# Differential attention in an encoder layer: the second softmax's factor computed on GpSimd instead of VectorE, and other planned waits around it

## The chip, the cores and the metric

The kernel runs on one core of a Trainium2 chip. The metric is the device time of one execution in microseconds (us); lower is better. The engines of the core are named as in the profile: PE is TensorE's matmul pipe, PEld its weight loads, DVE is VectorE, ACT is ScalarE, POOL is GpSimd and SP is SyncE, which here only issues transfers.

## The reference

One layer of an encoder trunk with 512 tokens and 1024 channels: a norm, one wide input projection, three branches (pooling, differential attention, a bidirectional recurrence) with gates, an output projection, then a SwiGLU feed-forward network and a final norm. The change lies in the attention branch alone:

```python
def diff_attention(q, k, v, lam, gain, lambda_init):
    # 4 heads, each with 2 softmaxes over 512 keys; query blocks of 128
    ...
        s = jnp.einsum('bqhcd,bkhcd->bhcqk', qblk, k) * scale
        s = s - slopes[:, None, None, None] * dist
        p = jax.nn.softmax(s, axis=-1)
        a = (p[:, :, 0] - lam * p[:, :, 1]).astype(v.dtype)
        return jnp.einsum('bhqk,bkhe->bqhe', a, v)
    ...
    o = rms_norm(o, gain) * (1.0 - lambda_init)
```

For each query row there are two sums of exponentials, z0 and z1. The kernel does not divide by z0 at this point: it forms e0 - lam * (z0 / z1) * e1 from the unnormalised exponentials e0 and e1, and lets 1/z0 enter later, inside the head's norm. The number -lam * z0 / z1, one for each row, is "the second softmax's factor"; in the code it is `co`.

## The kernel before, in words

Every matmul is done as three fp32r products of a high and a low part, so each weight block that arrives by DMA is split first: ACT writes the high part (`whi`, line 183) and DVE the low part (`wlo`, line 184). Both must be there before PE can use the block.

The attention stage works on four heads, and in each on four blocks of 128 queries. `scores(i)` (line 1046) issues, for each of the two softmaxes, two matmuls into a PSUM bank; one DVE operation adds the distances and takes the minimum (line 1056); one ACT operation takes the exponential and its row sum, which lands in `zz` (line 1058). Then DVE takes the reciprocals of the two sums (line 1062, `rr`), forms the factor (line 1064, `co`) and combines the two exponentials (line 1066). `turn(i)` (line 1069) transposes the result on PE in four pieces, and ACT and DVE copy it out of PSUM as high and low part (`aT`, lines 1075 and 1076). After four blocks, 12 matmuls multiply with the values (line 1097), and `head_norm` (line 647) squares the result, sums it with four small matmuls by `onesD` (line 657), passes through three small DVE operations, one power on POOL (line 140, called from line 666) and one more DVE operation, and ends with four transposes of `rso` (line 671).

The order of the matmuls is made when the program is built. Several generators run side by side under a planner (`Pipe`, line 39): the four heads, the pooling windows, and the stream of other jobs (`jobs.stream`: the projections of later heads, of the pooling branch `u`, and the `ups` of the recurrence), which fills the time between. A planned clock advances by a fixed price at each matmul (line 95) and transpose (line 100); a generator that yields `("w", t)` is taken up again t planned us later, and one that yields `("e", name, t)` waits until an event is marked. Waiting heads come before the job stream in the list, so a head goes on as soon as its wait is over, and the job stream takes what lies between. The job stream gives up control after every second matmul. PE keeps the order that the planner makes. The order on ACT, DVE and POOL is fixed at build time too, by a scheduler that models when each instruction becomes ready; on the chip each of these queues runs strictly in that order.

The waits of a head stand in lines 1080 and 1085: from one `turn` to the next `scores` 1.8, from `scores(i + 1)` to `turn(i)` 1.6. When the attention stage's job stream is used up, the next stage (line 1735: the pooling branch's mix, the gates' sums and differences `gsum`, and gate jobs) follows on PE.

Of the kernel before, what the change touches and what calls it, by code (L numbers as in the profile page):

```python
# [11 lines left out]
F32 = mybir.dt.float32  # L12
# [3 lines left out]
ALU = mybir.AluOpType  # L16
PSUM = bass.MemoryType.PSUM

P = 128
S = 512  # L20
D = 1024
NB = S // P
# [16 lines left out]
class Pipe:  # L39
# [8 lines left out]
    def mark(self, name):  # L48
        self.events[name] = self.t
# [27 lines left out]
def encoder_kernel(ctx: ExitStack, tc: tile.TileContext, x, norm1_g, w_in, pool_w, pool_scale,  # L77
# [3 lines left out]
    nc = tc.nc  # L81
# [3 lines left out]
    def pool(name, bufs=1, **kw):  # L85
        return tc.tile_pool(name=name, bufs=bufs, **kw)


    def mm(out_, lhsT, rhs, start, stop, chain=False):
        i = nc.tensor.matmul(out_, lhsT=lhsT, rhs=rhs, start=start, stop=stop, skip_group_check=chain)  # L90
        tc.keep_in_program_order(i)
        n = 1
        for d in rhs.shape[1:]:
            n *= d
        pipe.t += max(0.107, n * 0.0004167 + 0.002) if rhs.dtype == F32R else max(0.216, n * 0.001667 + 0.004)

    def transpose(out_, in_, idn):
        tc.keep_in_program_order(nc.tensor.transpose(out_, in_, idn))  # L98
        pipe.t += 0.108
# [8 lines left out]
    const = ctx.enter_context(pool("const"))  # L108
    wraw = ctx.enter_context(pool("wraw", 2))
    wsp = ctx.enter_context(pool("wsp", 3))  # L110
    small = ctx.enter_context(pool("small", 5))
    psum = ctx.enter_context(pool("psum", 3, space=PSUM))

    def bank(name, shape=(P, 512)):
        return psum.tile(list(shape), F32, name=name, bufs=2 if name == "tp" else 3)
# [7 lines left out]
    warmed = nc.scalar.activation(out=warm, in_=warm, func=AF.Exp).ins  # L123
    ident = const.tile([P, P], F32, name="ident")
    make_identity(nc, ident)
    onesD = const.tile([P, 1], F32, name="onesD")
    nc.vector.memset(onesD, 1.0 / P)
    mhalf = const.tile([P, 8], F32, name="mhalf")
    nc.vector.memset(mhalf, -0.5)
    masks = const.tile([P, len(LEVELS), P], U8, name="masks")  # L130
    vcol = const.tile([P, 14], F32, name="vcol")
    gain_a = const.tile([P, 1], F32, name="gain_a")
    lb = const.tile([P, 8], F32, name="lb")
    om = const.tile([P, 8], F32, name="om")
    nlam = const.tile([P, 1], F32, name="nlam")
# [3 lines left out]
    def pow_mhalf(dst, src):  # L139
        return nc.gpsimd.tensor_tensor(out=dst, in0=src, in1=mhalf[:, :src.shape[1]], op=ALU.pow).ins  # L140

    def rsqrt_eps(dst, mean):

        ms = small.tile([P, 8], F32, name="ms")[:, :mean.shape[1]]
        eng = nc.vector if mean.space == PSUM else nc.gpsimd
        eng.tensor_scalar(out=ms, in0=mean, scalar1=1.0, scalar2=EPS, op0=ALU.mult, op1=ALU.add)
        return pow_mhalf(dst, ms)
# [431 lines left out]
    ps = bank("mm")  # L579
# [67 lines left out]
    def head_norm(o_ps, tmp, gain, r0=None, bufs=2):  # L647


        og = tmp.tile([P, S], F32, name="og", bufs=bufs)  # L650
        sq = tmp.tile([P, S], F32, name="sqo", bufs=bufs)
        nc.scalar.activation(out=sq, in_=o_ps, func=AF.Square)
        nc.scalar.activation(out=og, in_=o_ps, func=AF.Copy, scale=gain)
        yield ("w", 1.3)
        sp = bank("tp")
        for b in range(NB):
            mm(sp[:, b:b + 1], sq[:, b * P:(b + 1) * P], onesD, True, True)
        r = small.tile([P, NB], F32, name="rso")
        if r0 is None:
            rsqrt_eps(r, sp[:, 0:NB])  # L660
        else:
            m = small.tile([P, NB], F32, name="mo")
            nc.vector.tensor_tensor(out=m, in0=sp[:, 0:NB], in1=r0, op=ALU.mult)
            nc.vector.tensor_tensor(out=m, in0=m, in1=r0, op=ALU.mult)
            nc.vector.tensor_scalar(out=m, in0=m, scalar1=EPS, scalar2=None, op0=ALU.add)
            pow_mhalf(r, m)
            nc.vector.tensor_tensor(out=r, in0=r, in1=r0, op=ALU.mult)
        yield ("w", 3.55)
        rb = bank("tp")
        for b in range(NB):  # L670
            transpose(rb[:, b * P:(b + 1) * P], r[:, b:b + 1].to_broadcast([P, P]), ident)
        return og, rb
# [359 lines left out]
    def att_head(h):  # L1032
        if h:
            yield ("e", f"QK{h - 1}", 0.0)
        if h > 1:
            yield ("e", f"AN{h - 2}", 0.0)
        yield ("e", f"AF{h}", 6.0)
        t = att.pop(h)
        at, (vh, vl), aT, y_attn = ATT["at"], ATT["v"], ATT["aT"], ATT["y"]
        strip = ATT["strip"].tile([P, 896], F32, name="strip")  # L1040
        nc.sync.dma_start(out=strip, in_=c_dist[h])
        zz = at.tile([P, NB, 2], F32, name="zz")
        rr = at.tile([P, NB, 2], F32, name="rr")
        probs = {}

        def scores(i):
            bs = slice(i * P, (i + 1) * P)
            mx = small.tile([P, 2], F32, name="mx")
            ex = []
            for c in range(2):  # L1050
                ps = bank("rc")
                mm(ps, t[f"q{c}"][:, bs], t[f"k{c}"], True, False)
                mm(ps, t[f"q{c}"][:, bs], t[f"l{c}"], False, True)
                s = at.tile([P, S], F32, name=f"s{c}")

                nc.vector.tensor_tensor_reduce(out=s, in0=strip[:, 384 - P * i:896 - P * i], in1=ps, scale=1.0,  # L1056
                                               scalar=3.0e38, op0=ALU.add, op1=ALU.min, accum_out=mx[:, c:c + 1])
                nc.scalar.activation(out=s, in_=s, func=AF.Exp, scale=-1.0, bias=mx[:, c:c + 1],  # L1058
                                     accum_out=zz[:, i, c:c + 1])
                ex.append(s)  # L1060

            nc.vector.reciprocal(out=rr[:, i, :], in_=zz[:, i, :])
            co = small.tile([P, 1], F32, name="co")
            nc.vector.scalar_tensor_tensor(out=co, in0=zz[:, i, 0:1], scalar=nlam, in1=rr[:, i, 1:2],
                                           op0=ALU.mult, op1=ALU.mult)
            nc.vector.scalar_tensor_tensor(out=ex[0], in0=ex[1], scalar=co, in1=ex[0], op0=ALU.mult, op1=ALU.add)  # L1066
            probs[i] = ex[0]

        def turn(i):
            bs = slice(i * P, (i + 1) * P)  # L1070
            p = probs.pop(i)
            pt = bank("tp", (P, NB, P))
            for k in range(NB):
                transpose(pt[:, k, :], p[:, k * P:(k + 1) * P], ident)
            nc.scalar.copy(out=aT[0][:, :, bs], in_=pt)
            nc.vector.tensor_tensor(out=aT[1][:, :, bs], in0=pt, in1=aT[0][:, :, bs].bitcast(F32), op=ALU.subtract)

        scores(0)
        for i in range(NB):
            yield ("w", 1.8 + (0.7 if i == 0 else 0.0))  # L1080
            if i + 1 < NB:
                scores(i + 1)
            else:
                mark(f"QK{h}")
            yield ("w", 1.6 + (1.0 if i + h == 0 else 0.0))
            if h and i == 0:
                yield ("e", f"PV{h - 1}", 0.0)
            turn(i)
        mark(f"T{h}")
        yield ("e", "VA", 1.5)  # L1090
        yield ("w", 1.5)
        ps = bank("rc")
        es = slice(h * P, (h + 1) * P)
        terms = [(vh, aT[0]), (vl, aT[0]), (vh, aT[1])]
        for i, (a, r) in enumerate(terms):
            for k in range(NB):
                mm(ps, a[:, k, es], r[:, k, :], i == 0 and k == 0, i == 2 and k == NB - 1)
            yield
        mark(f"PV{h}")
        og, rbp = yield from head_norm(ps, at, gain_a, rr[:, :, 0], 1)  # L1100
        mark(f"AN{h}")
        nc.vector.tensor_tensor(out=og, in0=og, in1=rbp, op=ALU.mult)
        nc.scalar.copy(out=y_attn[0][:, h, :], in_=og)
        nc.vector.tensor_tensor(out=y_attn[1][:, h, :], in0=og, in1=y_attn[0][:, h, :].bitcast(F32),
                                op=ALU.subtract)
# [725 lines left out]
```

## Time and profile before

| what | value |
|---|---|
| median of 3 runs | 886.92 us (886.86 to 887.57) |
| the profiled execution's own time | 886.27 us |
| its span, first to last instruction | 884.5 us |
| mean granted TensorE clock | 0.997 |
| PE busy | 867.9 us, 98% of the span |
| DVE busy | 664.5 us, 75% |
| ACT busy | 448.4 us, 51% |
| POOL busy | 18.7 us, 2%, 35 instructions |

The profiled execution lies 1.77 us above its own span and 0.65 us below the median of the runs. A row of the timeline gives the start in us, the duration in us, the engine, the line, the operation, "output<-inputs", the shapes and how many instructions were merged; in square brackets stands how long the engine was idle before it and who released it. Matmuls are pipelined, so their rows overlap by a fraction of a us. The heads are counted from 0; "block 3.0" is head 3, query block 0. The attention stage lies between about 218 us and 345 us of the span.

### The profile page before, as it was taken

The numbers are of one execution on the slowest core, as the hardware profiler recorded it, in microseconds if no ns is written. First come the engines' busy times: TensorE is split into PE (matmuls) and PEld (weight loads), VectorE is DVE, ScalarE is ACT, GpSimd is POOL, SyncE is SP. The second block draws the span as 40 slices with busy tenths as digits, with TensorE's granted clock in tenths as the row PEclk, the third lists the DMA queues.
The fourth block names the chain that finished last, engine by engine and source line by source line (L and its number), as shares of the span: only waits on it lengthen the run. The fifth ranks groups of instructions, "written<-read, shape, count | busy, mean of one in ns | idle before, by whom it ended". The sixth has DMA issues, their size and how long they took to land.

```text
span 884.5 us, 14079 instructions
## 1 busy us (share of the span) xinstructions
PE 867.9 (98%) x5713; PEld 786.7 (89%) x5713; DVE 664.5 (75%) x1005; ACT 448.4 (51%) x718; POOL 18.7 (2%) x35
## 2 busy tenths in 40 slices
PE   8999999999999989999999999999999999999996
PEld 7989988888998867899999898999999999988885
DVE  6788664844857876987877555998888888747996
ACT  6544343434746743553455334755555655533463
POOL 1000000000000000000000001000000000000001
PEclk9999999999999999999999999999999999999999
DMA  8330113024123311334331770153443443355002
GB/s 243 96 120 24 49 48 116 27 73 141 49 88 94 94 61 49 96 96 137 101 97 48 262 191 1 49 143 96 125 115 96 123 118 97 119 190 189 2 1 96
DMA packets 115693, 87.53 MB, mean 99 GB/s; under 512 B 3862, under 2 KB 104748, under 8 KB 115628
## 3 DMA queue, kind: packets, MB, share of 16 engines
q1 hardware_dynamic: 115036, 85.57, 32.0%
q8 instruction: 45, 0.74, 0.3%
q10 hardware_dynamic: 592, 1.05, 0.3%
q14 instruction: 20, 0.16, 0.1%
HBM read 84.52 MB, written 2.10 MB: 98 GB/s over the span
## 4 chain that ended last, share of the span: by engine, by line
PE 87%; DVE 7%; DMA 2%; issue 1%; ACT 1%; POOL 0%; SPq 0%; POOLq 0%; DVEq 0%; ACTq 0%
PE mm L90 58%; PE rc L90 26%; PE tp L90 2%; PE tp L98 1%; DVE wlo L184 1%; DMA raw<-in_w_out_dram 1%; DMA raw<-in_w_in_dram 1%; DVE hid L354 1%; DVE flo L354 1%; DMA xin<-in_x_dram 0%; DVE s L1066 0%; DVE win L1159 0%; DVE hrow L481 0%; DVE h_lo L498 0%; PE rc L98 0%
## 5 line engine op out<-in xcount | busy, mean ns | idle before, releaser
L183 ACT CAST whi<-raw 128x1024 fp32r<-128x1024 f32 (+1 forms) x134 | 127.5, 958 | 138.4 <-PE mm L90 88.6
L184 DVE TENSOR_TENSOR wlo<-raw,whi 128x1024 fp32r<-128x1024 f32 (+1 forms) x134 | 147.6, 1106 | 58.2 <-ACT whi L183 35.5
L90 PE MATMUL mm<-hT_hi,whi 128*128 128x512 f32 (+1 forms) x344 | 82.1, 371 | 0.0
L90 PE MATMUL mm<-hT_hi,wlo 128*128 128x512 f32 (+1 forms) x344 | 81.7, 370 | 0.2 <-DVE wlo L184 0.2
L90 PE MATMUL mm<-hT_lo,whi 128*128 128x512 f32 (+1 forms) x344 | 81.5, 372 | 0.0
L302 DVE TENSOR_TENSOR slo<-sums,shi 128x1024 fp32r<-128x1024 f32 x58 | 70.5, 1218 | 0.2 <-ACT shi L300 0.2
L90 PEld LDWEIGHTS mm<-hT_lo,whi 128*128 128x128 f32 x344 | 60.0, 191 | 9.9
L90 PEld LDWEIGHTS mm<-hT_hi,whi 128*128 128x128 f32 x344 | 58.9, 189 | 9.9 <-ACT hT_hi L494 0.4
L90 PEld LDWEIGHTS mm<-hT_hi,wlo 128*128 128x128 f32 x344 | 58.5, 188 | 9.5 <-DVE wlo L184 0.4
L300 ACT CAST shi<-sums 128x1024 fp32r<-128x1024 f32 x58 | 61.0, 1053 | 4.1 <-DVE sums L264 3.7
L261 DVE TENSOR_TENSOR sums<-raw 128x1024 f32<-128x1024 f32 x29 | 35.4, 1219 | 1.7 <-DMA raw<-in_w_in_dram 1.6
L90 PE MATMUL mm<-y_arena,whi 128*128 128x512 f32 x128 | 32.8, 394 | 0.0
L90 PE MATMUL mm<-whi,y_arena 128*128 128x256 f32 (+1 forms) x192 | 31.9, 315 | 0.4 <-ACT whi L183 0.2
L914 DVE TENSOR_TENSOR kq<-kq,pyr 128x256 f32<-128x256 f32 x48 | 18.2, 421 | 18.2 <-PE rc L90 18.2
L90 PE MATMUL rc<-kq,kc 128*128 128x128 f32 x224 | 31.6, 284 | 0.0
L90 PEld LDWEIGHTS rc<-kq,kc 128*128 128x128 f32 x224 | 30.1, 191 | 1.5
L1058 ACT ACTIVATE s<-s,mx 128x512 f32<-128x512 f32 x32 | 23.0, 720 | 16.7 <-DVE mx L1056 16.5
L90 PEld LDWEIGHTS mm<-whi,y_arena 128*128 128x128 f32 x192 | 27.4, 188 | 3.5 <-ACT whi L183 1.0
L883 ACT COPY kc<-kq 128x512 f32<-128x512 f32 x28 | 18.6, 666 | 20.2 <-PE rc L90 12.6
L90 PEld LDWEIGHTS mm<-y_arena,whi 128*128 128x128 f32 x128 | 23.7, 188 | 5.1
L1346 DVE TENSOR_TENSOR g<-mm,g 128x256 f32<-128x256 f32 x21 | 8.9, 424 | 23.7 <-PE mm L90 23.7
L90 PE MATMUL mm<-fhi,slo 128*128 128x256 f32 x168 | 26.1, 277 | 0.5 <-DVE slo L302 0.5
(383 smaller groups left out, 2031.5 us busy)
## 6 DMA issues: line engine op xcount, KB each, us to landing
raw<-in_w_in_dram SPq DMA_DIRECT2D x44, 512.0 KB, 4.2
raw<-in_w_ffn_in_dram SPq DMA_DIRECT2D x44, 512.0 KB, 5.3
raw<-in_w_in_dram SPq DMA_DIRECT2D x8, 1024.0 KB, 5.2
raw<-in_w_ffn_out_dram SPq DMA_DIRECT2D x7, 1024.0 KB, 5.0
raw<-in_w_out_dram SPq DMA_DIRECT2D x4, 1024.0 KB, 11.1
xin<-in_x_dram SPq DMA_DIRECT2D x4, 512.0 KB, 4.6
raw<-in_w_up_rec_dram SPq DMA_DIRECT2D x2, 1024.0 KB, 6.4
raw<-in_w_up_pool_dram SPq DMA_DIRECT2D x2, 1024.0 KB, 5.1
```

The lines of the kernel that those rows point to most:

```text
L90: i = nc.tensor.matmul(out_, lhsT=lhsT, rhs=rhs, start=start, stop=stop, skip_group_check=chain)
L98: tc.keep_in_program_order(nc.tensor.transpose(out_, in_, idn))
L183: nc.scalar.copy(out=hi, in_=view)
L184: LAST["wlo"] = nc.vector.tensor_tensor(out=lo, in0=view, in1=hi.bitcast(F32), op=ALU.subtract).ins
L261: nc.vector.tensor_tensor(out=strided(sums, 0, [[2 * half, 2], [1, half]]), in0=strided(self.raw, 0, [[3 * half, 2], [1, half]]), in1=stri ...
L300: nc.scalar.copy(out=hi, in_=view)
L302: on_dve = nc.vector.tensor_tensor(out=lo, in0=view, in1=hi.bitcast(F32), op=ALU.subtract).ins
L354: last[0] = form(**kw).ins
L883: nc.scalar.copy(out=strided(kc, 0, [[2 * n, S // (2 * n)], [n, 2], [1, n]]), in_=strided(kq, 2 * S, [[2 * n, S // (2 * n)], [S + n, 2], [ ...
L914: nc.vector.tensor_tensor(out=xv, in0=xv, in1=tv, op=ALU.mult)
L1058: nc.scalar.activation(out=s, in_=s, func=AF.Exp, scale=-1.0, bias=mx[:, c:c + 1], accum_out=zz[:, i, c:c + 1])
L1346: on_dve = nc.vector.tensor_tensor(out=c["g"], in0=c["x"], in1=c["g"], op=ALU.add).ins
```

## The change

The factor's two DVE operations go. In their place stand three POOL operations: z0 times -lam (`zn`), z1 to the power -1, and the product of the two. The reciprocals of the first sums, which the head's norm needs, are taken once for the whole head after its last `turn`. A constant column of -1 is filled once at the start, beside `onesD` in one tile, and `zn` and `co` share one tile, so that the tiles take the same room as before. The planned waits become 1.6 and 2.4.

```diff
-    onesD = const.tile([P, 1], F32, name="onesD")
+    fixed = const.tile([P, 2], F32, name="fixed")
+    onesD, minus1 = fixed[:, 0:1], fixed[:, 1:2]
     nc.vector.memset(onesD, 1.0 / P)
+    nc.vector.memset(minus1, -1.0)
...
-        rr = at.tile([P, NB, 2], F32, name="rr")
+        rr = at.tile([P, NB], F32, name="rr")
...
-            nc.vector.reciprocal(out=rr[:, i, :], in_=zz[:, i, :])
-            co = small.tile([P, 1], F32, name="co")
-            nc.vector.scalar_tensor_tensor(out=co, in0=zz[:, i, 0:1], scalar=nlam, in1=rr[:, i, 1:2],
-                                           op0=ALU.mult, op1=ALU.mult)
+            co = small.tile([P, 2], F32, name="co")
+            zn, co = co[:, 0:1], co[:, 1:2]
+            nc.gpsimd.tensor_tensor(out=zn, in0=zz[:, i, 0:1], in1=nlam, op=ALU.mult)
+            nc.gpsimd.tensor_tensor(out=co, in0=zz[:, i, 1:2], in1=minus1, op=ALU.pow)
+            nc.gpsimd.tensor_tensor(out=co, in0=co, in1=zn, op=ALU.mult)
             nc.vector.scalar_tensor_tensor(out=ex[0], in0=ex[1], scalar=co, in1=ex[0], op0=ALU.mult, op1=ALU.add)
...
-            yield ("w", 1.8 + (0.7 if i == 0 else 0.0))
+            yield ("w", 1.6 + (0.7 if i == 0 else 0.0))
             if i + 1 < NB:
                 scores(i + 1)
             else:
                 mark(f"QK{h}")
-            yield ("w", 1.6 + (1.0 if i + h == 0 else 0.0))
+            yield ("w", 2.4 + (1.0 if i + h == 0 else 0.0))
...
         mark(f"T{h}")
+        nc.vector.reciprocal(out=rr, in_=zz[:, :, 0])
...
-        og, rbp = yield from head_norm(ps, at, gain_a, rr[:, :, 0], 1)
+        og, rbp = yield from head_norm(ps, at, gain_a, rr, 1)
```

## The prediction, made before the changed kernel was run

> **What bounds the kernel now.** I read the page first, then PE's waits over the whole run, then windows and timelines of the stretch that the change touches. On the page:
>
> ```profile
> span 884.5 us, 14079 instructions
> ## 1 busy us (share of the span) xinstructions
> PE 867.9 (98%) x5713; PEld 786.7 (89%) x5713; DVE 664.5 (75%) x1005; ACT 448.4 (51%) x718; POOL 18.7 (2%) x35
> ```
>
> PE is busy 98% of the span, and the change adds or removes no matmul. So the time can move only by what PE idles, and by the clock it is granted. PE's waits, longest first, name three that belong to attention:
>
> ```profile
> PE tp L98 <- DVE s L1066: 2.8, 1, 2.8
> ...
> PE tp L98 <- DVE rr L1062: 1.0, 1, 1.0
> ...
> PE tp L98 <- DVE rso L667: 0.6, 1, 0.6
> ```
>
> Windows of the stage (after the length: busy us of PE, PEld, DVE, ACT, POOL, then the granted clock) show where they lie:
>
> ```profile
> 305.00:325.00 20.00, 18.99 (x97) 15.69 (x96) 16.82 (x44) 11.39 (x26) 1.01 (x1) 1.00 0.37 119
> 325.00:345.00 20.00, 16.65 (x75) 13.46 (x74) 10.34 (x26) 5.77 (x8) 1.56 (x1) 0.91 0.16 53
> ...
> 329.00:331.00 2.00, 1.25 (x5) 1.25 (x6) 0.60 (x1) 0.13 (x1) 0.00 (x0) 0.54 0.00 0
> 331.00:333.00 2.00, 2.00 (x7) 1.56 (x6) 0.69 (x1) 0.46 (x1) 0.00 (x0) 0.61 0.00 0
> ```
>
> The idle time is all in head 3, and after the long wait the granted clock falls to 0.54 and 0.61 for some 4 us. PE's timeline gives the places:
>
> ```profile
> 304.66 1.08 PE L90 MATMUL rc<-aT_hi,va_hi 128*128 128x512 f32 x4
> ...
> 311.25 0.63 PE L98 MATMUL tp<-ident,s 128*128 128x128 f32 x4 [1.01 <-DVE rr L1062]
> ...
> 320.41 0.61 PE L90 MATMUL mm<-y_arena,whi 128*128 128x512 f32 x2
> ...
> 322.23 0.60 PE L98 MATMUL tp<-ident,s 128*128 128x128 f32 x4
> ...
> 324.06 1.09 PE L90 MATMUL mm<-y_arena,wlo 128*128 128x512 f32 x4
> 324.98 1.98 PE L90 MATMUL mm<-hT_hi,whi 128*128 128x512 f32 x8
> 329.75 1.09 PE L98 MATMUL tp<-ident,s 128*128 128x128 f32 x4 [2.79 <-DVE s L1066]
> 330.49 3.06 PE L90 MATMUL mm<-hT_lo,whi 128*128 128x512 f32 x8
> ...
> 337.95 0.95 PE L90 MATMUL tp<-onesD,sqo 128*128 128x1 f32 x8
> ...
> 343.69 0.62 PE L98 MATMUL tp<-ident,rso 128*128 128x128 f32 x4 [0.56 <-DVE rso L667]
> ```
>
> The transposes of block 3.0 wait 1.01 us, those of 3.3 2.79, those of head 3's norm 0.56: 4.36 together. At the low clock the transposes of 3.3 take 1.09 instead of 0.60 and the next eight matmuls 3.06 instead of 1.98: 1.57 more. **5.93 us** is what the stage can win.
>
> The Trainium skill, "TensorE: Matmul & The Clock Gate", Part 1, lets the clock fall to one half after an idle window of about 3.4 us. Here it fell behind 2.79 us of idling, so I count the 1.57 to the stall; by that page's figure the two need not hang together, and the forecast would be up to 1.57 us higher.
>
> **The planned waits.** `scores(i)` and `turn(i)` have between them two waits of line 1085, one of line 1080 and one `turn`: 2 x 1.6 + 1.8 = 5.0 planned us before, 2 x 2.4 + 1.6 = 6.4 after. The job stream fills the 1.4 us with six matmuls at 0.215 each. On the chip one takes 0.23 (four start at 324.06, the next at 324.98), so each transpose has about **1.38 us** more until PE reaches it. Stepping the planner's arithmetic through this stage with the old waits gives the order that the timeline shows; with the new ones it gives six more in 3.0 and 3.3, five to eight more in the other blocks from 1.2 on, and in head 0 0.7 to 1.65 us worth of half-width ones. Only the first two blocks of head 1 lose, one to two us of some twenty.
>
> The price is at the end. Each block takes 0.6 planned us longer, so head 3 ends later against a job stream that is no longer than before. Between the sums of head 3's norm (line 657) and its `rso` transposes stood 18 matmuls; 12 are left, and nothing follows before the next stage. That wait has 1.38 us less cover.
>
> **The factor on POOL.** What goes is quoted by the groups:
>
> ```profile
> L1064 DVE SCALAR_TENSOR_TENSOR co<-zz,nlam,rr 128x1 f32<-128x1 f32 x16 | 3.5, 218 | 0.4
> ...
> L1062 DVE RECIPROCAL rr<-zz 128x2 f32<-128x2 f32 x16 | 2.6, 162 | 5.1 <-ACT s L1058 4.9
> ```
>
> That is 6.1 us of DVE, less four reciprocals (about 0.16 each). No stretch is bound by DVE's total, so this counts nothing by itself. What counts is the delay from the exponential's sum to the combination. For block 0.0, with DVE free, it is 224.12 - 223.64 = 0.48 us:
>
> ```profile
> 223.45 0.19 ACT L1058 ACTIVATION_READ_ACCUMULATOR s<-s,mx 128x1 f32 x1
> ...
> 224.12 0.75 DVE L1066 SCALAR_TENSOR_TENSOR s<-s,co,s 128x512 f32<-128x512 f32 x1
> ```
>
> For POOL the rows are a one-input operation, a power on one column, and powers on four columns in the norm:
>
> ```profile
> 5.68 0.20 POOL L146 TENSOR_SCALAR ms<-ss 128x1 f32<-128x1 f32 x1 [1.02 <-ACT hrow L475]
> 5.96 0.56 POOL L140 TENSOR_TENSOR rstd<-ms,mhalf 128x1 f32<-128x1 f32 x1
> ...
> 262.95 1.01 POOL L140 TENSOR_TENSOR rso<-mo,mhalf 128x4 f32<-128x4 f32 x1 [61.88 <-DVE mo L665]
> ...
> 341.79 0.69 DVE L1168 SCALAR_TENSOR_TENSOR gate<-win,gate 128x512 f32<-128x512 f32 x1
> 341.79 1.56 POOL L140 TENSOR_TENSOR rso<-mo,mhalf 128x4 f32<-128x4 f32 x1 [29.23 <-DVE win L1166]
> 343.38 0.16 DVE L667 TENSOR_TENSOR rso<-rso,rr 128x4 f32<-128x4 f32 x1 [0.90 <-POOL rso L140]
> ```
>
> `zn` needs only the first sum and is done before the second. A power costs 0.56. A two-input product on one column is not in the trace: bounds 0.20 (one input) and 0.56 (the power); three more columns of power cost 0.45, so one column is 0.15 and what is left is 0.41, which I take. One POOL operation follows another by 0.08 (5.88 to 5.96); I use that for the step from ACT too, and 0.03 to DVE (343.35 to 343.38). Undisturbed: 0.08 + 0.56 + 0.08 + 0.41 + 0.03 = 1.16 us, 0.68 more than 0.48. The power at 341.79 took 0.55 longer than that at 262.95, beside a DVE operation with two SBUF inputs; DVE does much of that here (lines 184, 1066, 1159), so I add 0.55 once: **1.71 us**, bounds 0.95 (the product at 0.20, nothing beside it) and, with two long DVE operations in front, 3.6.
>
> **Block 3.3.** The old chain in detail:
>
> ```profile
> 324.68 0.19 ACT L1058 ACTIVATION_READ_ACCUMULATOR s<-s,mx 128x1 f32 x1
> ...
> 325.61 0.15 DVE L1062 RECIPROCAL rr<-zz 128x2 f32<-128x2 f32 x1
> ...
> 326.39 1.22 DVE L184 TENSOR_TENSOR wlo<-raw,whi 128x1024 fp32r<-128x1024 f32 x1
> 327.52 0.21 DVE L1064 SCALAR_TENSOR_TENSOR co<-zz,nlam,rr 128x1 f32<-128x1 f32 x1
> ...
> 328.86 0.75 DVE L1066 SCALAR_TENSOR_TENSOR s<-s,co,s 128x512 f32<-128x512 f32 x1
> ```
>
> The sums were there at 324.87, but DVE's queue put other work between reciprocal, factor and combination, which began at 328.86: 3.99 us for 0.48 of need. After the change there is one place for such work, ahead of the combination. From the end of the scores (320.41): 4.46 to the sums, 0.46 more because the cast behind 3.2's transposes stands ahead of them on ACT and comes two matmuls later, 1.71, one `wlo` (1.22) in front of the combination, 0.75, and 0.14 to PE: 8.74. PE arrives after 329.75 - 2.79 - 320.41 = 6.55 + 1.38 = 7.93. Stall **0.81** instead of 2.79; too short, I take it, for the clock.
>
> **Block 3.0.** From 304.66, the old time to the sums is 4.81:
>
> ```profile
> 309.27 0.20 ACT L1058 ACTIVATION_READ_ACCUMULATOR s<-s,mx 128x1 f32 x1
> ```
>
> With 0.46 (the norm's ACT work stands ahead, two matmuls later), 1.71, 0.75, 0.14 it is 7.87; PE arrives after 311.25 - 1.01 - 304.66 + 1.38 = 6.96. Stall **0.91** instead of 1.01.
>
> **Head 3's norm.** From 338.90 to 343.69 the old wait is 4.79, of which matmuls covered 4.23; 2.85 will be covered. If the chain stays, the stall is 1.94. But in it DVE put the third pooling window between each two small steps and disturbed the power. After the change that window's input is ready earlier: the planner ends `u2` before the value matmuls. Free of it, from the sums to the power 0.68 (head 0 below, 262.27 to 262.95), power 1.01, 0.03 + 0.16, 0.15 to PE: 2.03. I add one `wlo`: 3.25, stall **0.40**, bounds 0 and 1.94.
>
> ```profile
> 261.32 0.95 PE L90 MATMUL tp<-onesD,sqo 128*128 128x1 f32 x8
> ```
>
> The next-tightest transposes are 1.3's, 0.50 us behind their combination; with 1.38 - 0.68 - 0.55 they keep 0.65:
>
> ```profile
> 273.80 0.75 DVE L1066 SCALAR_TENSOR_TENSOR s<-s,co,s 128x512 f32<-128x512 f32 x1
> 275.05 0.60 PE L98 MATMUL tp<-ident,s 128*128 128x128 f32 x4
> ```
>
> The added memset of -1 lies in the first microseconds, where POOL itself idles 1.02 us for ACT at 5.68; if not hidden it costs a tenth.
>
> **Sum.** 0.81 + 0.91 + 0.40 = 2.12 against 5.93: 3.81 us less. 886.27 - 3.81 = 882.46 for the profiled execution; the median stood 0.65 above it: **883.1 us**.
>
> **Rivals.** First: the queue of DVE, not the factor, holds the combination, and the late head gives the gain back. With 3.99 kept in 3.3 the chain is 4.46 + 0.46 + 3.99 + 0.75 + 0.14 = 9.80, stall 1.87; 3.0 0.91; norm 1.94: 4.72, with the clock's 1.57 at most 6.29. That is 885.7 to 887.3. For it speaks that DVE's order is made anew and the tail has less cover; against it, that two of three links leave DVE.
>
> Second, slower: POOL is held up. POOL's three operations each wait while DVE reads two SBUF inputs, and DVE then waits in order for `co`, with `wlo` and the next minimum queued behind it, for which PE and ACT wait. Let the delay beyond 1.16 be X. Stalls: 3.3 X - 0.96, 3.0 X + 0.36, 1.3 X - 1.20, norm 1.94. At X = 1.93 they equal 5.93. With two `wlo` in front, X = 2.44: 1.48 + 2.80 + 1.24 + 1.94 + 1.57 (2.80 drops the clock) = 9.03, that is 890.0 us. For it speaks the 1.56 at 341.79; against it, that the page shows POOL free for 98% of the span, and that most operations around the sums (line 1056, line 1076) read PSUM.
>
> The Trainium skill names the same conflict: "GPSIMD Engine Reference", section 1, has POOL share its SBUF interfaces with VectorE and lists two-SBUF-input instructions as contending. The trace agrees in the power that took 1.56.
>
> Third: the change does little, because DVE's freed time is worth nothing; that is the first rival's outcome.
>
> **How the numbers follow.** I give the forecast 0.65, the first rival 0.22, the second 0.13. The forecast spans from all stalls gone (886.92 - 5.93 = 881.0) to 885.1. A change of 0.2%, 1.77 us, is about what a measurement of this kernel can tell from none: below 885.15 is faster, above 888.69 slower. The range runs from 881.0 to 887.4, the upper end of the first rival.
>
> **What would show it.** In the changed profile: six more matmuls between scores and transposes; no wait of 2.8 us at 3.3 and no clock below 1 near 330 us; POOL's `co` within 1.2 to 1.7 us of the sums; DVE some 5 us less busy; a wait for `rso` under 1 us at the last head. It is wrong if a transpose still waits over 2 us for line 1066, if POOL's operations stretch past 1 us each, or if a new PE wait appears elsewhere.

## The result, and the profile after

The changed kernel takes **881.16 us** (median of 6 runs, 880.80 to 882.01) where the kernel before took 886.89 us (6 runs, 885.29 to 887.57). The ratio is 0.9939, with a 95% interval of 0.9926 to 0.9952: 5.73 us less. The profiled execution took 880.92 us with a span of 879.0 us, 5.5 us shorter than the span before.

In the changed kernel's file the lines have moved: the exponential is L1060, POOL's three operations are L1066 (`zn`), L1067 (the power) and L1068 (the product), the combination is L1069, the cast and the rest of a turned block L1078 and L1079, the weight split L185 and L186, the cast of `l` L1025, the norm's small steps L665 to L669 with its power at L142.

The page of the changed kernel, the same lines as before:

```profile
span 879.0 us, 14111 instructions
## 1 busy us (share of the span) xinstructions
PE 866.3 (99%) x5713; PEld 786.4 (89%) x5713; DVE 660.8 (75%) x978; ACT 448.9 (51%) x718; POOL 37.8 (4%) x83
```

PE has the same 5713 matmuls and is busy 1.6 us less, the low clock's share. DVE is busy 3.7 us less, with 27 instructions fewer; POOL has 48 more, three for each of 16 blocks, and 19.1 us more of work.

PE's waits of the changed kernel in the attention stage (total us, count, longest): all three of before are gone, and this one is new:

```profile
PE rc L90 <- ACT l L1025: 0.8, 1, 0.8
```

The windows of head 3 in the changed kernel (length; busy us of PE, PEld, DVE, ACT, POOL; granted clock): PE is busy all through both, and the clock that was 0.91 in the second is 1.00:

```profile
305.00:325.00 20.00, 20.00 (x102) 16.52 (x101) 17.48 (x42) 12.60 (x26) 5.64 (x11) 1.00 0.38 119
325.00:345.00 20.00, 20.00 (x97) 16.65 (x96) 14.32 (x26) 8.42 (x14) 2.26 (x3) 1.00 0.16 53
```

PE's timeline of the changed kernel at the same three places, and at head 2's first scores, where the new wait is:

```profile
279.18 0.50 PE L90 MATMUL rc<-l,q 128*128 128x512 f32 x1 [0.81 <-ACT l L1025]
...
312.45 0.60 PE L98 MATMUL tp<-ident,s 128*128 128x128 f32 x4
...
321.60 1.98 PE L90 MATMUL mm<-y_arena,whi 128*128 128x512 f32 x8
...
329.36 0.60 PE L98 MATMUL tp<-ident,s 128*128 128x128 f32 x4
...
339.86 0.60 PE L98 MATMUL tp<-ident,rso 128*128 128x128 f32 x4
```

None of the three rows of transposes has an idle time in brackets any more, and each takes 0.60 us, the time at full clock. Block 3.3 has 329.36 - 321.60 = 7.76 us between the end of its scores and its transposes (6.55 before until PE arrived).

So the account of the two profiled executions closes: 5.93 us of stalls and low clock went, 0.81 came, which is 5.12 of the 5.5 by which the spans differ. The other 0.4 is within the spread of the changed kernel's own runs, whose spans go from 878.9 to 880.2 us.

The chain of block 3.3 in the changed kernel, as rows of the timeline:

```profile
326.00 1.22 DVE L186 TENSOR_TENSOR wlo<-raw,whi 128x1024 fp32r<-128x1024 f32 x1
326.30 0.19 ACT L1060 ACTIVATION_READ_ACCUMULATOR s<-s,mx 128x1 f32 x1
...
326.57 1.05 POOL L1067 TENSOR_TENSOR co<-zz,fixed 128x1 f32<-128x1 f32 x1 [1.82 <-ACT s L1060]
...
327.13 0.68 DVE L1179 TENSOR_TENSOR pwlo<-pw,pwhi 128x512 fp32r<-128x512 f32 x1
327.70 0.19 POOL L1068 TENSOR_TENSOR co<-co 128x1 f32<-128x1 f32 x1
327.74 0.68 DVE L1079 TENSOR_TENSOR aT_lo<-tp,aT_hi 128x512 fp32r<-128x512 f32 x1
328.34 0.74 DVE L1069 SCALAR_TENSOR_TENSOR s<-s,co,s 128x512 f32<-128x512 f32 x1
```

The sums are there at 326.49, 4.89 us after the scores; the power takes 1.05 instead of 0.56, the product 0.19, and `co` is there at 327.89, 1.40 us after the sums. The combination begins 1.85 us after the sums (3.99 before). DVE runs without a break until then: a `wlo` that had begun before the sums, a `pwlo` and an `aT_lo`. So for the last 0.45 us it is again DVE's queue that holds the combination, and not the factor. The combination ends at 329.08, and the transposes follow 0.28 us later without having waited. Where they do wait, this step takes 0.14 (3.3 in the kernel before), so 0.14 us is to spare.

### The profile page after: what moved, and what is told of

The parts are those of the page before. It is cut to its first block, busy times and chain, and to the rows that moved or that the text cites. A ratio compares the mean times of both kernels' runs of the same rounds, so it can differ in the third digit from the quotient of the medians.

```text
span 879.0 us, 14111 instructions
## 1 busy us (share of the span) xinstructions
PE 866.3 (99%) x5713; PEld 786.4 (89%) x5713; DVE 660.8 (75%) x978; ACT 448.9 (51%) x718; POOL 37.8 (4%) x83
## 3 DMA queue, kind: packets, MB, share of 16 engines
q10 hardware_dynamic: 592, 1.05, 0.3%
## 4 chain that ended last, share of the span: by engine, by line
PE 86%; issue 7%; DVE 3%; DMA 2%; ACT 1%; POOL 1%; POOLq 0%; DVEq 0%; ACTq 0%
PE mm L90 56%; PE rc L90 26%; PE tp L90 2%; PE tp L98 2%; DMA raw<-in_w_out_dram 1%; DVE wlo L186 1%; DVE hrow L483 1%; DMA raw<-in_w_in_dram 0%; ACT whi L185 0%; DVE hT_lo L500 0%; PE rc L98 0%; ACT s L1060 0%; POOL rso L142 0%; DVE g1b L577 0%; ACT l L1025 0%
## 5 line engine op out<-in xcount | busy, mean ns | idle before, releaser
L185 ACT CAST whi<-raw 128x1024 fp32r<-128x1024 f32 (+1 forms) x134 | 127.6, 958 | 141.5 <-PE mm L90 90.7
L186 DVE TENSOR_TENSOR wlo<-raw,whi 128x1024 fp32r<-128x1024 f32 (+1 forms) x134 | 147.5, 1106 | 51.2 <-ACT whi L185 35.4
L1060 ACT ACTIVATE s<-s,mx 128x512 f32<-128x512 f32 x32 | 23.1, 721 | 10.9 <-DVE mx L1058 10.7
```

The costliest lines, as they stand in the source:

```text
L185: nc.scalar.copy(out=hi, in_=view)
L186: LAST["wlo"] = nc.vector.tensor_tensor(out=lo, in0=view, in1=hi.bitcast(F32), op=ALU.subtract).ins
```

## The experiments

Each was run beside the kernel before on the same chip, five times (the one with two links eleven times). Theory **W** says that the longer planned waits, the cover, bring the gain; theory **Q** that it comes from taking two links of the chain out of DVE's queue, into which that queue put other work. The rivals of the prediction are that the queue still holds the combination, and that POOL is held up.

**The waits alone.** The kernel before, factor on DVE, with the new waits:

```diff
-            yield ("w", 1.8 + (0.7 if i == 0 else 0.0))
+            yield ("w", 1.6 + (0.7 if i == 0 else 0.0))
...
-            yield ("w", 1.6 + (1.0 if i + h == 0 else 0.0))
+            yield ("w", 2.4 + (1.0 if i + h == 0 else 0.0))
```

> The kernel before with the new planned waits (1.6 and 2.4) alone; the factor stays on VectorE. Theory W (the longer cover between scores and transposes does it): block 3.0 no longer waits (1.01 less 1.38 of cover), 3.3 waits about 1.4 instead of 2.79 and the clock stays up, so that with the 0.8 us wait that the new order brings at head 2's scores the time is 883.2 to 885.2 us. Theory Q (taking two links out of VectorE's queue does it): the old chain of 3.99 us stays and the late head costs 1.4, so 886 to 888 us, and the transposes of 3.3 still wait 2 us or more.

Measured: 881.41 us against 886.76, ratio 0.9942 (0.9930 to 0.9954). That is the changed kernel's time, without POOL, and 1.8 us below the fast end of what W was expected to give: no wait is left at 3.3, where 1.4 us was expected. In PE's waits of the attention stage one is left, at head 2's scores:

```profile
PE rc L90 <- ACT l L1023: 0.4, 1, 0.4
```

The cover is not all that the new waits bring. With them the planner issues everything in another order, and DVE's queue comes out otherwise too. Block 3.3 of this kernel:

```profile
325.56 1.21 DVE L184 TENSOR_TENSOR wlo<-raw,whi 128x1024 fp32r<-128x1024 f32 x1
326.09 0.19 ACT L1058 ACTIVATION_READ_ACCUMULATOR s<-s,mx 128x1 f32 x1
...
326.73 0.68 DVE L1175 TENSOR_TENSOR pwlo<-pw,pwhi 128x512 fp32r<-128x512 f32 x1
...
327.33 0.15 DVE L1062 RECIPROCAL rr<-zz 128x2 f32<-128x2 f32 x1
327.40 0.67 DVE L1076 TENSOR_TENSOR aT_lo<-tp,aT_hi 128x512 fp32r<-128x512 f32 x1
327.99 0.21 DVE L1064 SCALAR_TENSOR_TENSOR co<-zz,nlam,rr 128x1 f32<-128x1 f32 x1
...
328.23 0.75 DVE L1066 SCALAR_TENSOR_TENSOR s<-s,co,s 128x512 f32<-128x512 f32 x1
```

Only one long operation stands between the links, and the `wlo` and the `pwlo` lie ahead of the reciprocal: from the sums at 326.28 to the combination 1.95 us instead of 3.99. The transposes begin at 329.13, 0.15 after the combination's end, about what the step takes where they wait: nothing is to spare. With 3.99 kept they would have waited about 2.0 us in spite of the cover (3.99 - 1.95), an estimate from these rows. So the new waits are enough, but by cover and order together; this run doesn't part the two.

**GpSimd alone.** The changed kernel with the old waits (1.6 and 2.4 put back to 1.8 and 1.6):

```diff
-            yield ("w", 1.6 + (0.7 if i == 0 else 0.0))
+            yield ("w", 1.8 + (0.7 if i == 0 else 0.0))
...
-            yield ("w", 2.4 + (1.0 if i + h == 0 else 0.0))
+            yield ("w", 1.6 + (1.0 if i + h == 0 else 0.0))
```

> The changed kernel with the old planned waits (1.8 and 1.6); the factor on GpSimd. Theory Q: the chain from sums to combination stays at the 0.9 to 2.0 us that the changed kernel shows, so 3.3 waits about 0.6 and 3.0 nothing, and the time is 881.5 to 883.5 us. Theory W: without the six matmuls of cover the longer chain of GpSimd makes waits of its own, 3.3 waits 2 us or more again, and the time is 885 to 888 us.

Measured: 882.17 us against 886.76, ratio 0.9953 (0.9940 to 0.9965). Its waits:

```profile
PE tp L98 <- DVE mo L666: 1.0, 1, 1.0
PE tp L98 <- DVE s L1069: 0.4, 1, 0.4
```

At 3.3 the delay from sums to combination is 1.59 us and PE waits 0.39 instead of 2.79, at the old cover and with the sums as late after the scores as before (4.45 us). At 3.3 too it is DVE's queue that holds the combination: `co` is there at 326.68, the combination begins at 327.34, behind a merge. At 3.0, where no wait was expected, PE still waits 1.04, because there the sums are late (310.32) and not the factor (0.93 later). The profile puts that wait down to `mo`, but the combination ends at 312.00 and the transposes follow 0.15 us later. The norm's wait of 0.56 is gone as well: the power there begins at 338.85, 0.09 us ahead of the window's last operation, and takes 1.02 us; in the kernel before the two begin together, at 341.79, and it takes 1.56. So GpSimd alone takes 4.6 us off and the waits alone take 5.35, and both together 5.73: they remove the same stall, and their gains don't add.

**The order on VectorE alone.** This is the test of Q without its engine. PE, ACT, POOL and the DMA queues issue in the order of the kernel before, the factor stays on DVE, and only in block 3.3 the factor and the combination stand ahead of the merges, the pooling window's two last steps, the `wlo` and the `pwlo`, most of which stood between the links. `hold()` only orders an instruction behind the combination of that block:

```diff
+    def hold():
+        return tc.issue_after(LAST["combined"]) if "combined" in LAST else ExitStack()
...
-        LAST["wlo"] = nc.vector.tensor_tensor(out=lo, in0=view, in1=hi.bitcast(F32), op=ALU.subtract).ins
+        with hold(): LAST["wlo"] = nc.vector.tensor_tensor(out=lo, in0=view, in1=hi.bitcast(F32), op=ALU.subtract).ins
...
-                nc.vector.tensor_tensor(out=merged[:, dt, :], in0=ps, in1=sg, op=ALU.mult)
+                with hold(): nc.vector.tensor_tensor(out=merged[:, dt, :], in0=ps, in1=sg, op=ALU.mult)
...
```

> The kernel before, factor on VectorE, old waits, the same order on PE, ACT, GpSimd and SyncE; only on VectorE, in block 3.3, the factor and the combination stand ahead of two merges, the window's end, the two low parts and the memsets that stood between them. If the queue between the links is the cause of the 2.79 us, the chain of 3.99 us falls to 0.5 to 1.2, 3.3 does not wait, the clock stays up and 4.4 us go: 882.2 to 882.8 us; the 1.0 of 3.0 and the 0.6 or more of the last norm stay. If the longer cover is what is needed, 3.3 still waits 1.5 us or more and the time is 885 us or more. The work put behind may come too late for PE: then a new wait appears and takes back up to 2 us.

Measured: 882.12 us against 886.52, ratio 0.9952 (0.9939 to 0.9964). 4.4 us less, and 2.79 + 1.57 = 4.36 was the stall at 3.3 with its low clock. The chain, the waits and the window of this kernel:

```profile
325.33 0.15 DVE L1062 RECIPROCAL rr<-zz 128x2 f32<-128x2 f32 x1
...
325.52 0.22 DVE L1064 SCALAR_TENSOR_TENSOR co<-zz,nlam,rr 128x1 f32<-128x1 f32 x1
325.77 0.75 DVE L1066 SCALAR_TENSOR_TENSOR s<-s,co,s 128x512 f32<-128x512 f32 x1
...
327.73 1.21 DVE L184 TENSOR_TENSOR wlo<-raw,whi 128x1024 fp32r<-128x1024 f32 x1
```

```profile
PE tp L98 <- DVE rr L1062: 1.0, 1, 1.0
PE tp L98 <- DVE rso L667: 0.6, 1, 0.6
```

```profile
325.00:345.00 20.00, 19.44 (x95) 15.94 (x94) 13.95 (x30) 7.32 (x12) 1.55 (x1) 1.00 0.18 56
```

The three links now follow one another, 0.57 us from the sums to the combination, the `wlo` comes behind them, the wait at 3.3 is gone and the clock stays at 1.00. The waits at 3.0 and at the norm are untouched. ACT and POOL show the same order of operations in the attention stage as before, and PE comes no later. This shows the cause of the largest term directly: the wait came from what DVE's queue had between the links. Neither more cover nor another engine for the factor was needed to remove it.

**Two links, old waits.** The changed kernel also takes one column out of each reciprocal. If any small edit of that kind would have redrawn DVE's order, this would show it; two links of the old chain (reciprocal and factor) stay on DVE:

```diff
-            nc.vector.reciprocal(out=rr[:, i, :], in_=zz[:, i, :])
+            nc.vector.reciprocal(out=rr[:, i, 1:2], in_=zz[:, i, 1:2])
...
+        nc.vector.reciprocal(out=rr[:, :, 0], in_=zz[:, :, 0])
```

> The kernel before with the reciprocals of the first sums taken once for each head; the factor stays two links on VectorE (the first of them one column instead of two), old waits. It gives next to nothing by its own cost (16 reciprocals of one column instead of two, four more of four), but lets the scheduler make VectorE's order anew. If the 3.99 us in block 3.3 are owed to the two links as such, 3.3 still waits 2 us or more: 886 to 888 us. If they are one draw of the order among many, the wait may go or shrink: 882 to 885 us.

Measured: 887.11 us against 886.52, ratio 1.0003 (0.9994 to 1.0012). The delay at 3.3 is 4.07 us, and PE waits there as before:

```profile
PE tp L98 <- DVE s L1066: 2.9, 1, 2.9
PE tp L98 <- DVE rr L1062: 1.0, 1, 1.0
PE tp L98 <- DVE rso L667: 0.6, 1, 0.6
```

So what removed the wait at 3.3 in the run with GpSimd alone was not the edit of the reciprocal, but the factor's leaving DVE, with the order of DVE's queue that came with it.

**Head 2's scores later.** The changed kernel with its new wait of 0.81 us taken away: head 2's first scores are planned one us later.

```diff
-        yield ("e", f"AF{h}", 6.0)
+        yield ("e", f"AF{h}", 7.0 if h == 2 else 6.0)
```

> The changed kernel with head 2 starting one planned us later (7.0 instead of 6.0 behind its projections), which puts six more matmuls ahead of its first scores. If the 0.81 us wait of those scores for ACT's cast of the low part of k is a real loss, it goes and the time is 880.2 to 880.6 us. Rival: head 3 then ends two matmuls later, and its norm, or 3.3 with 0.28 us to spare, gives it back: 881.0 to 881.6 us.

Measured: 880.91 us against 886.76, ratio 0.9935 (0.9921 to 0.9949). The wait is gone, and PE doesn't idle at all between 205 and 365 us. The median lies between the two expected ranges, 0.25 us below the changed kernel's, less than its runs spread.

**The same on VectorE.** The first experiment's waits, and head 2's scores one us later, with the factor on DVE:

```diff
-        yield ("e", f"AF{h}", 6.0)
+        yield ("e", f"AF{h}", 7.0 if h == 2 else 6.0)
...
-            yield ("w", 1.8 + (0.7 if i == 0 else 0.0))
+            yield ("w", 1.6 + (0.7 if i == 0 else 0.0))
...
-            yield ("w", 1.6 + (1.0 if i + h == 0 else 0.0))
+            yield ("w", 2.4 + (1.0 if i + h == 0 else 0.0))
```

> The new planned waits with the factor on VectorE, and head 2 starting one planned us later: the factor's place is the only difference to the run in which head 2 starts later with the factor on GpSimd (880.91 us). If the cover alone is the gain, the two are equal within the noise: 880.6 to 881.3 us. If taking the links off VectorE is worth something beside the cover, this is slower by 0.5 us or more: 881.4 to 882.5 us.

Measured: 880.51 us against 886.52, ratio 0.9929 (0.9917 to 0.9942); no wait is left in attention. Beside 880.91 with POOL the difference is within the runs' spread: where the cover is there, these runs show no difference between the two engines of the factor. The two were measured on different chips; a pair from one chip stands below.

**New waits in head 3 only.** The kernel before, factor on DVE:

```diff
-            yield ("w", 1.8 + (0.7 if i == 0 else 0.0))
+            yield ("w", (1.6 if h == 3 else 1.8) + (0.7 if i == 0 else 0.0))
...
-            yield ("w", 1.6 + (1.0 if i + h == 0 else 0.0))
+            yield ("w", (2.4 if h == 3 else 1.6) + (1.0 if i + h == 0 else 0.0))
```

> The kernel before with the new planned waits in head 3 alone. All three waits before lay in head 3, so if the cover is what counts there and nowhere else, nearly the whole gain comes from this: 881.0 to 882.0 us, with no wait at head 2's scores. If the waits in the other heads matter too (by VectorE's order at the start of head 3), 3.0 still waits up to 1 us: 882.0 to 883.5 us.

Measured: 880.42 us against 886.52, ratio 0.9934 (0.9922 to 0.9947), no wait in attention. The cover is needed in head 3 alone, and where the other heads keep their order, head 2's scores don't come too early. At 3.0 this run tests the cover by itself: the sums come 4.81 us after the scores and the combination 0.90 after the sums, as before (4.81 and 0.89), and four more matmuls ahead of the transposes take the listed wait of 1.01 us away. Nothing is to spare there either: the transposes begin 0.15 us after the combination's end. At 3.3 more than the cover has changed. The delay at 3.3 is 2.89 us here, more than in the changed kernel, and it is covered: the sums come 2.98 us after the scores, since ACT's order is another as well.

Run once more, on another chip:

> The kernel before with the new waits in head 3 alone once more, factor on VectorE: 880.4 us again if this version beats the changed kernel by the 0.8 us wait of head 2's scores; 881.0 us or more if the first result was a lucky one.

Measured: 881.55 us against 887.02, ratio 0.9940 (0.9927 to 0.9952). By that expectation the first result was a lucky one.

**The changed kernel with new waits in head 3 only.** The same edit on the changed kernel:

```diff
-            yield ("w", 1.6 + (0.7 if i == 0 else 0.0))
+            yield ("w", (1.6 if h == 3 else 1.8) + (0.7 if i == 0 else 0.0))
...
-            yield ("w", 2.4 + (1.0 if i + h == 0 else 0.0))
+            yield ("w", (2.4 if h == 3 else 1.6) + (1.0 if i + h == 0 else 0.0))
```

> The changed kernel with the new waits in head 3 alone: the factor's place is the only difference to the run with these waits and the factor on VectorE (880.42 us). If the place of the factor is worth nothing once the cover is there, 880.2 to 881.0 us. If the longer chain on GpSimd costs where heads 0 to 2 have the old cover, a wait appears at 2.0, 2.2 or 1.3 (0.15 to 0.78 us to spare with the factor on GpSimd and the old waits) and the time is 881 to 882 us. If it helps, 880.0 us or less.

Measured: 880.90 us against 887.02, ratio 0.9933 (0.9921 to 0.9946), no wait in attention. On the same chip the same waits with the factor on DVE took the 881.55 above, and the runs of the two overlap (880.00 to 881.71 here, 880.38 to 882.11 there): no gain or loss by the factor's engine is shown. And the changed kernel itself beside it, without an edit:

> The changed kernel itself once more, beside the run above on the same chip: 881.2 us, from 880.8 to 882.0, so that the two can be compared without the other runs of before.

Measured: 881.30 us against 887.02, ratio 0.9939 (0.9926 to 0.9953). These last six runs lie between 880.4 and 881.6, and one kernel measured twice came out 1.1 us apart (880.42 and 881.55). None of them is shown to be faster than the changed kernel.

**The factor delayed.** The second rival's price, put in by hand. The changed kernel with four more powers of -1 between the first power and the product; an even number of them gives the same value back, so that only time is added:

```diff
             nc.gpsimd.tensor_tensor(out=co, in0=zz[:, i, 1:2], in1=minus1, op=ALU.pow)
+            nc.gpsimd.tensor_tensor(out=co, in0=co, in1=minus1, op=ALU.pow)
+            nc.gpsimd.tensor_tensor(out=co, in0=co, in1=minus1, op=ALU.pow)
+            nc.gpsimd.tensor_tensor(out=co, in0=co, in1=minus1, op=ALU.pow)
+            nc.gpsimd.tensor_tensor(out=co, in0=co, in1=minus1, op=ALU.pow)
             nc.gpsimd.tensor_tensor(out=co, in0=co, in1=zn, op=ALU.mult)
```

> The changed kernel with four more powers to -1 behind the first in GpSimd's chain (the value is the same up to rounding), 4 x (0.56 + 0.08) = 2.56 us more delay of the factor. By the prediction's second rival each transpose waits by what its spare time in the changed profile does not cover: 3.3 2.42, 3.0 1.30, 2.0 1.08, 0.0 0.93, 1.3 0.61, 2.3 0.18: up to 6.5 us, 885 to 888 us, with a low clock behind the longest. Rival: VectorE's order is made anew around the later factor, so that only 3.3 waits: about 883.5 us. If nothing waits, the delay of the factor has no part in the result.

Measured: 891.85 us against 886.76, ratio 1.0058 (1.0045 to 1.0071); the span is 9.9 us longer than the changed kernel's, more than was expected. From the sums to the combination it now takes 3.5 to 5.7 us. PE's waits for the combination, its timeline and the clock in this kernel:

```profile
PE tp L98 <- DVE s L1073: 6.3, 3, 2.8
```

```profile
228.84 0.66 PE L98 MATMUL tp<-ident,s 128*128 128x128 f32 x4 [1.62 <-DVE s L1073]
...
317.37 1.08 PE L98 MATMUL tp<-ident,s 128*128 128x128 f32 x4 [2.79 <-DVE s L1073]
318.10 2.91 PE L90 MATMUL mm<-hT_lo,whi 128*128 128x512 f32 x6
...
338.70 0.63 PE L98 MATMUL tp<-ident,s 128*128 128x128 f32 x4 [1.86 <-DVE s L1073]
339.09 1.18 PE L90 MATMUL mm<-hT_hi,wlo 128*128 128x512 f32 x4
```

```profile
317.00:319.00 2.00, 1.63 (x6) 1.57 (x7) 0.22 (x1) 0.51 (x1) 1.75 (x4) 0.50 0.00 0
...
340.00:342.00 2.00, 2.00 (x11) 1.61 (x10) 2.00 (x3) 0.59 (x1) 0.00 (x0) 1.00 0.04 8
```

Block 0.0 waits 1.62 us, 3.0 2.79, 3.3 1.86, and with the 2.79 the clock falls to 0.50, so that six matmuls take 2.91 us. In these three blocks the combination comes 2.1 to 3.5 us later after the sums than in the changed kernel. So the rival's mechanism exists: PE does come to wait when the factor is that late. In the changed kernel it costs nothing, at 3.0 with 1.26 us to spare (1.40 less the step of 0.14). At 3.3 only 0.14 is to spare, but there DVE's queue holds the combination for 0.45 us beyond `co` anyway, so that by these rows a factor up to about 0.6 us later would cost nothing.

## Why the prediction was right, and where its sizes were off

The direction and the mechanism were right: the stage could win 5.93 us, the wait at 3.3 and its low clock were the main part, and DVE's queue, with other work between the links, was the cause of that wait. The run with only DVE's order changed in 3.3 shows this. The measured gain is 5.73 us where 3.81 was forecast, and 881.16 lies only 0.16 us inside the fast end of the range, the end at which all stalls are gone. The step that was mis-sized is the sum of the stalls that stay, 0.81 + 0.91 + 0.40 = 2.12: all three were 0, and a new wait of 0.81 came in at head 2's scores.

The cover came as planned: six more matmuls stand between scores and transposes at 3.0 and 3.3. The count 5.0 to 6.4 of the prediction holds for blocks 1 to 3 of a head, though; the first block has one wait of line 1085 only, and its six at 3.0 come from the planner as a whole, which the prediction had stepped through.

**Block 3.3, forecast 0.81, measured 0 with 0.14 to spare.** The arrival of PE held (7.93, measured 7.76; the prediction took the end of a row of matmuls for the start of the next, and the rows overlap by 0.17). That of the sums held by luck (4.92, measured 4.89): the prediction had the cast behind 3.2's transposes ahead of the exponentials, but in the trace it comes behind them, at 326.39, and two other casts, a `whi` at 324.22 and the `pwhi` at 325.16, stand between the two exponentials. The factor was forecast at 1.71 and a `wlo` behind it at 1.22, 2.93 in all; they took 1.40 and 0.45, together 1.85. The product cost 0.19, not 0.41: of the two bounds the one-input operation was the right neighbour, not the remainder of the power. And in front of the combination stood an `aT_lo`, which had begun 0.15 us before `co` was there and held the combination for another 0.45 us. The `wlo` ran earlier, beside the power.

**The power's contention, forecast 0.55 in each block.** The groups of the changed kernel's stage (busy, mean ns, then the idle time before them) show what POOL's operations took:

```profile
L1067 POOL TENSOR_TENSOR co<-zz,fixed 128x1 f32<-128x1 f32 x16 | 12.3, 771 | 12.6 <-ACT s L1060 12.6
L1069 DVE SCALAR_TENSOR_TENSOR s<-s,co,s 128x512 f32<-128x512 f32 x16 | 12.0, 750 | 7.5 <-POOL co L1068 5.8 <-ACT whi L185 1.4
...
L1066 POOL TENSOR_TENSOR co<-zz,nlam 128x1 f32<-128x1 f32 x16 | 3.9, 243 | 75.2 <-ACT s L1060 75.0
...
L1068 POOL TENSOR_TENSOR co<-co 128x1 f32<-128x1 f32 x16 | 3.1, 193 | 1.3
```

The mean power is 0.77 us, 0.22 above the 0.55 of one alone; 3.3, at 1.05, had nearly the 0.55 that was added. DVE did idle 5.8 us for `co` in the sixteen blocks together, at no cost to PE.

**Block 3.0, forecast 0.91, measured 0 with 1.26 to spare.** The sums were expected 5.27 us after the scores' end, because the norm's ACT work of head 2 stood ahead of the exponentials. They came 3.33 us after it (305.62 to 308.95), for in the new order that work stands behind them, at 309.01. And the factor took 1.35 us, not 1.71. I carried the old order of ACT over into the new plan; it was made anew. With GpSimd alone, where the old order stays, 3.0 does wait its 1.04 us.

**Head 3's norm, forecast 0.40, measured 0.** That the third pooling window is out of the way before the norm's small steps was right: DVE idles 1.72 us ahead of them, and the power takes 1.02 us, undisturbed. The `wlo` of 1.22 that I added begins at 340.11, behind the chain's end, and not within it:

```profile
337.18 0.17 DVE L665 TENSOR_TENSOR mo<-tp,rr 128x4 f32<-128x4 f32 x1 [1.72 <-PE tp L90]
...
338.88 0.16 DVE L669 TENSOR_TENSOR rso<-rso,rr 128x4 f32<-128x4 f32 x1 [1.13 <-POOL rso L142]
340.11 1.23 DVE L186 TENSOR_TENSOR wlo<-raw,whi 128x1024 fp32r<-128x1024 f32 x1 [1.06 <-PE mm L90]
```

**What was not foreseen** is the wait of 0.81 us at head 2's first scores. The planner now issues them 6.03 of its us after the projections, 8.2 before, and ACT has a weight cast ahead of the cast of `l` that they read:

```profile
277.44 1.05 ACT L185 CAST whi<-raw 128x1024 fp32r<-128x1024 f32 x1
278.51 0.62 ACT L1025 CAST l<-l 64x512 fp32r<-64x512 f32 x1
```

I had asked only who loses cover between scores and transposes, and not whose input is read earlier. The prediction named a new PE wait elsewhere as a sign of error; this one is small and costs at most what it shows.

**DVE some 5 us less busy** was forecast, 3.7 measured. Nothing hung on it.

**The rivals.** The first, that the queue still holds the combination and the late head gives the gain back, did not come about as a loss: with the new waits no wait in head 3 is left, with the factor on either engine. Its mechanism is there at 3.3, but holds the combination 0.45 us beyond `co` and not 3.99 beyond the sums. The second is a real mechanism but not at this delay. That the two parts of the change do the same work twice was no rival of mine, and should have been one: it is what the first two experiments show. At 3.0 cover alone is enough, as the new waits in head 3 show. What stays open is how much of the waits-only gain at 3.3 is cover and how much is the order that DVE got with it.

## What to carry to other kernels

Count the links of a dependent chain on a busy engine that works in order: between any two of them the queue may hold a long operation of other work, and here 0.48 us of need took 3.99. Then the cheapest cure may be to place the links next to one another, or to give the consumer more to do in one place; moving a link to an idle engine cures the same wait, and the gains don't add. After any change of an issue order, look for consumers that are now issued earlier, and read each queue's order anew instead of carrying the old one over.

## What was not expected of the hardware

The clock fell with PE's idle times of 2.79 us (the kernel before, and the kernel with the delayed factor) and 2.86 us (two links, old waits: 0.91 in the mean of 325 to 345 us). It did not fall with 1.86 and 1.62 us. But the length of the idle time doesn't set the moment. In windows of 0.1 us the granted clock drops 2.2 us into the idling in the kernel before (at 329.16), 1.1 us into it with the delayed factor (315.65), and with the two links only at 331.32, 1.1 us after PE had resumed. It then stayed at 0.50 for 3.4, 6.8 and 3.4 us. So these five idle times give no threshold. The Trainium skill, "TensorE: Matmul & The Clock Gate", Part 1, gives an idle window of about 3.4 us; these runs saw the fall with shorter idle times, and 3.4 us, once or twice over, as the time that the low clock lasted.

A product of two columns on POOL took 0.19 us when nothing disturbed it, as little as an operation with one input (0.20), where a power takes 0.55. The longest power ran beside a DVE operation with two inputs in SBUF, in the changed kernel's block 3.2:

```profile
317.73 1.64 POOL L1067 TENSOR_TENSOR co<-zz,fixed 128x1 f32<-128x1 f32 x1 [0.52 <-ACT s L1060]
317.74 1.23 DVE L186 TENSOR_TENSOR wlo<-raw,whi 128x1024 fp32r<-128x1024 f32 x1 [0.43 <-ACT s L1060]
```

It lost 1.09 us, nearly the whole of the 1.23 us beside it, as though it had stood still meanwhile. The other fifteen powers of this profile fit: six more began while a DVE operation with two SBUF inputs was running (a `wlo`, or the window's last step), and each lost the overlap less 0.12 to 0.15 us: 0.41 of 0.55, 0.50 of 0.65, 0.62 of 0.76. Nine took 0.55 or 0.56, with nothing beside them or an operation that reads PSUM; the one at 246.47 ran wholly beside an `aT_lo`. And with GpSimd alone the norm's power, which began 0.09 us ahead of such a DVE operation, lost nothing (1.02). So in these traces a power that began behind such a DVE operation, or with it (0.01 us apart at 317.73), stood still for most of the rest of it, and one that began 0.09 us ahead did not.
